# A matrix-valued causal convolution: other buffers for the first partial results

## The chip, the cores and the metric

The kernel runs on one core of a Trainium2 chip. The core has engines that run side by side, each with its own queue of instructions: TensorE (PE in the profile) multiplies matrices into PSUM, VectorE (DVE) and ScalarE (ACT) work elementwise, GpSimd (POOL) and SyncE (SP) issue transfers here. Engines wait for each other and for transfers by semaphores. The metric is the time of one execution on the device in microseconds, the median of several runs.

## The reference

```python
x: (8, 4096, 512) float32,  kernel: (8, 512, 512) float32
out = 0
for k in range(8):
    shifted = x moved down by k rows within its sequence, zeros ahead
    out += shifted @ kernel[k]
```

Each output row is the sum of eight products of a row of 512 with a 512 x 512 matrix: the row itself and the seven before it. It is a convolution along the sequence whose taps are matrices.

## The kernel before, in words

The 8 x 4096 rows are cut into 128 runs of 256 rows. A run belongs to a partition; a step is the same row of all 128 runs. Eight steps make a group, with index `i` from 0 to 31 (`NIT`), so that a group's outputs are 8 steps of 128 x 512.

The eight taps are not multiplied out one by one. A three-level scheme in the manner of Karatsuba splits taps and steps into a low and a high half at each level (`LO`, `HI`) and forms a third set (`MID`) from sums of inputs and differences of weights. Inputs are combined on VectorE in bfloat16 (`D4`, `D42`, `D421`, `D41`, `D2`, `D21`, `D1`, and in the opening `T4`, `T42`, `E4`, `F0`, `F21`, `A1`, `C0`, `C1`). A product (`product`, line 188) is 4 matmuls of 128x128 by 128x512 on one 128 x 512 half of a PSUM tile.

The work is a list of nodes, `order` (line 305). A node (i, a) is group `i` and outer level `a`; it makes the sums `p[0]` and `p[1]`, two steps each, in PSUM. On one node's way lie `node_a1`, `node_a0`, `node_u` (products in the tile `q`), ScalarE's copies of `q` as a start value (`node_seed`, lines 249 and 251) and into `dts` (line 255), `node_v` (a product each for b = 0 and 1), `node_d` (VectorE makes the other half of `p` from it, lines 263 and 265) and `node_l` (the last products). `node_e` takes the result out of PSUM. For a MID node from the third group on, ScalarE copies `p` into a tile `ms` (line 292), and the LO and HI nodes of that group add or subtract it on VectorE into a tile `y` (line 301) that is stored by SyncE (`store`, line 275).

The first six nodes go another way, since MID needs weights that come late: the order is (0, LO), (1, LO), (0, HI), (1, HI), (0, MID), (1, MID). Nodes 0 to 3 copy their `p` into tiles kept in `first` (line 288); when nodes 4 and 5 have their sums, `node_y` (line 279) adds them in place and the tiles are stored. They are stored in this order: the first group's LO and HI with b = 0 (lines 517 and 524), with b = 1 (533 and 540), then the second group's LO and HI with b = 0 (544 and 546), HI with b = 1 (556) and LO with b = 1 (559).

The tiles of `first` come from three pools (lines 194 to 197): `ms` has two buffers, `f` two, `y` four. A pool hands its buffers out in turn. Whoever takes a buffer again first waits until its last reader, here a store, is done. `f` is not used after the opening. So the pool that a node's results lie in decides on which store node 6 (the first to fill `ms` again) and nodes 7 and 8 (the first to fill `y` again) have to wait.

Everything is put in order by hand (`manual_schedule`, line 54): each engine runs its instructions in the order in which the program names them, up to line 559 one by one and from line 562 in a loop over the nodes from the seventh. SyncE issues both stores and the transposing transfers into `XT` (`transpose_x`, line 89); GpSimd loads `x` and the weights (line 80). In the opening a part of the input is transposed on TensorE instead (`transpose_pe`, line 179), and `direct(m, t)` (line 315) does the products of node 0 one by one.

Of the kernel before, what the change touches and what calls it, by code (L numbers as in the profile page):

```python
# [22 lines left out]
def kernel(  # L23
# [6 lines left out]
    nc = tc.nc  # L30
# [10 lines left out]
    ADD = mybir.AluOpType.add  # L41
# [26 lines left out]
    D21 = spool.tile([P, 4, D], bf, name="D21")  # L68
# [3 lines left out]
    F0 = spool.tile([P, D], bf, name="F0")  # L72
    A1 = spool.tile([P, 2, D], bf, name="A1")

    def tt(o, a, b, op):
        nc.vector.tensor_tensor(out=o, in0=a, in1=b, op=op)  # L76


    def load(out, src):
        nc.gpsimd.dma_start(out=out, in_=src)  # L80
# [3 lines left out]
    def load_x(i, h):  # L84
        xin[i, h] = xpool.tile([P, 4, D], bf, name="xin")
        load(xin[i, h], xr[:, K * i + 4 * h:K * i + 4 * h + 4, :])

    def transpose_x(i, h):
        nc.sync.dma_start_transpose(
            out=XT[:, 4 * h:4 * h + 4, :].rearrange("p j (c m) -> p (j c) m", m=P),  # L90
            in_=xin[i, h].rearrange("p j d -> p (j d)"))
# [20 lines left out]
    def prep_d41(h):  # L112
        if h == LO:
            tt(D41[:, 0:2], D4[:, 7::-7], D4[:, 0:2], ADD)
        else:
            tt(D41[:, 2:4], D4[:, 3:5], D4[:, 4:6], ADD)
# [18 lines left out]
    def pair(k):  # L135
        return ppool.tile([P, 2, D], f32, name=f"pp{k}")
# [4 lines left out]
    H, HF = XT, D421.bitcast(f32).rearrange("p (t b) d -> p t (b d)", b=2)  # L141
# [18 lines left out]
    def mid_dve(*which):  # L160
        o, u, v = mid(*which)
        tt(o, u, v, SUB)
# [12 lines left out]
    def transpose_pe(name, k, src, t0, t1):  # L175
        o = pair(k).bitcast(bf).rearrange("p a (b d) -> p (a b) d", b=2)
        for t in range(t0, t1):
            for c in range(DC):
                nc.tensor.transpose(o[:, t - t0, c * P:(c + 1) * P], src[:, t, c * P:(c + 1) * P],  # L179
                                    ident)  # L180
        bank[name] = o[:, 0:t1 - t0]
# [3 lines left out]
    XF = D42  # L185


    def product(bank, comp, w, start):
        for c in range(DC):
            nc.tensor.matmul(bank, lhsT=comp[:, c * P:(c + 1) * P], rhs=w[:, c, :],  # L190
                             start=start and c == 0, stop=c == DC - 1,
                             skip_group_check=True)

    mpool = ctx.enter_context(tc.tile_pool(name="m", bufs=2))
    cpool = ctx.enter_context(tc.tile_pool(name="c", bufs=2))
    fpool = ctx.enter_context(tc.tile_pool(name="f", bufs=2))
    ypool = ctx.enter_context(tc.tile_pool(name="y", bufs=4))
# [31 lines left out]
    def node_a1(k):  # L229
        n = Node()  # L230
        nodes.append(n)
        n.k, (n.i, n.a) = k, order[k]
        a = n.a
        n.s = streams(n.i, a)
        n.q = pair(3)
        product(n.q[:, 1], n.s[1][1], W[a, MID, HI], True)
        nc.scalar.copy(out=n.q[:, 0], in_=n.q[:, 1])  # L237
        n.p = {}
# [4 lines left out]
    def node_u(n):  # L243
        product(n.q[:, 1], n.s[0], W[n.a, MID, MID], False)
# [23 lines left out]
    ms = {}  # L268
# [4 lines left out]
    def store(i, a, b_, y):  # L273
        t0 = K * i + 4 * a + 2 * b_
        nc.sync.dma_start(out=orr[:, t0:t0 + 2, :], in_=y)
# [7 lines left out]
    def node_e(n, b_):  # L283
        p = n.p[b_]
        if n.k < 4:
            pool, name = ((ypool, "y"), (mpool, "ms"), (ypool, "y"), (fpool, "f"))[n.k]
            y = pool.tile([P, 2, D], f32, name=name)
            nc.scalar.copy(out=y, in_=p)
            first[n.i, n.a, b_] = y
        elif n.a == MID:  # L290
            ms[b_] = mpool.tile([P, 2, D], f32, name="ms")
            nc.scalar.copy(out=ms[b_], in_=p)  # L292
        else:
            y = ypool.tile([P, 2, D], f32, name="y")
            if b_ == HI and n.k == len(order) - 1:

                for j, eng in enumerate((nc.scalar, nc.sync)):
                    tt(y[:, j], p[:, j], ms[b_][:, j], ADD if n.a == LO else SUB)
                    eng.dma_start(out=orr[:, K * n.i + 4 * n.a + 2 * b_ + j, :], in_=y[:, j])
            else:  # L300
                tt(y, p, ms[b_], ADD if n.a == LO else SUB)
                store(n.i, n.a, b_, y)
# [12 lines left out]
    def direct(m, t):  # L315
        n = K // 2 - 1 - m
        product(n0.p[t // 2][:, t % 2], D4[:, t - m] if t >= m else E4[:, 4 + t - m],
                W[LO, n >> 1, n & 1], m == 0)


    C0, C1 = W[MID, HI, MID], W[MID, LO, MID]

    def to(z):
        return z.rearrange("p t (c m) -> p t c m", m=P)[:, :, :, 1:P]

    def prev(z):
        return z.rearrange("p t (c m) -> p t c m", m=P)[:, :, :, 0:P - 1]

    def first_run(z):

        nc.vector.memset(z[:, :, 0:D:G], 0.0)
# [2 lines left out]

    nc.vector.tensor_copy(out=H[:, 4:6], in_=HF[:, 0:2])
    nc.scalar.copy(out=H[:, 6:8], in_=HF[:, 2:4])
    n0.p = {0: pair(0), 1: pair(1)}
    load_w(6)  # L340
# [21 lines left out]
    load_x(1, 0)  # L362
    tt(to(E4[:, 1:4]), prev(bank["he"]), to(XF[:, 1:4]), ADD)
    direct(2, 2)
    direct(0, 1)
    first_run(E4[:, 1:4])
    direct(1, 1)
    tt(D1, XF[:, 3:5], XF[:, 4:6], ADD)
    mid_dve(1, LO, HI)
    nc.vector.tensor_copy(out=F0, in_=XF[:, 4])  # L370
    mid_dve(2, LO, HI)
    tt(F21, D2[:, 0:4], D2[:, 1:5], ADD)
    direct(2, 0)
# [10 lines left out]
    tt(D4[:, 4:8], XF[:, 4:8], XT[:, 4:8], ADD)  # L384
    direct(1, 2)
    tt(D42[:, 3], D4[:, 1], D4[:, 3], ADD)
    transpose_pe("x2", 2, xin[1, 0], 0, 4)
    prep_d41(HI)
    direct(3, 2)
# [10 lines left out]
    tt(D41[:, 1], T4[:, 0], T4[:, 1], ADD)  # L400
    load_w(3)
    node_a1(1)
    direct(2, 1)
    node_u(nodes[1])
    tt(D41[:, 0], D4[:, 7], T4[:, 0], ADD)
    tt(T42[:, 0:2], D4[:, 6:8], T4[:, 0:2], ADD)
# [2 lines left out]
    mid_dve(1, HI, HI)  # L409
    load_w(1)  # L410
    node_e(nodes[0], 0)
    load_x(1, 1)
    load_x(2, 0)
# [8 lines left out]
    node_seed(nodes[1], 1)  # L422
    mid_dve(1, HI, LO)
    node_e(nodes[0], 1)
    mid_dve(2, HI, HI)
    node_v(nodes[1], 1)
# [6 lines left out]
    node_a1(2)  # L433
    node_l(nodes[1], 0, LO)
    node_e(nodes[1], 0)
    transpose_x(1, 1)
    node_a0(nodes[2])
# [45 lines left out]
    node_dts(nodes[4])  # L483
    tt(D21[:, 2:4], C1[:, 0:2], C1[:, 2:4], ADD)
    mid_dve(2, MID, MID)
    tt(D21[:, 0:2], C0[:, 0:2], C1[:, 0:2], ADD)
    tt(A1[:, 1], C1[:, 0], C1[:, 1], ADD)
    load_x(3, 0)
    transpose_x(2, 0)
    mid_dve(2, MID, LO)  # L490
    node_e(nodes[3], 0)
# [148 lines left out]
```

## Time and profile before

The median of three runs is 785.68 us (783.73 to 785.83). The profiled execution took 783.4 us, of which 781.4 us are its span.

| Engine | busy, us | share of the span |
|---|---|---|
| TensorE, matmuls | 761.4 | 97% |
| VectorE | 659.6 | 84% |
| TensorE, weight loads | 346.3 | 44% |
| ScalarE | 281.9 | 36% |

| Stretch, us | TensorE busy | VectorE busy |
|---|---|---|
| 0 to 200 | 187.4 | 170.0 |
| 200 to 400 | 199.0 | 169.2 |
| 400 to 600 | 199.1 | 171.1 |
| 600 to 781 | 176.0 | 149.3 |

The granted TensorE clock is full throughout. The 16 transfer engines moved 138.9 MB, 178 GB/s in the mean. A line of the timeline gives start, duration, engine, line of the kernel, operation, output and input tile, and in brackets how long the engine had stood idle and what released it. A line of waits gives the engine and line that waited, what for, the total, the number of waits and the longest. A releaser is inferred from semaphores: where several had to come, the last is named.

### The profile page before, as it was taken

How to read it: one execution, taken by the hardware profiler on the slowest of the kernel's cores; microseconds unless marked ns; L12 is line 12 of the kernel's file. 1: busy time of each engine (PE TensorE's matmuls, PEld its weight loads, DVE VectorE, ACT ScalarE, POOL GpSimd, SP SyncE). 2: the span in 40 equal slices, each digit the busy share in tenths (PEclk: the TensorE clock that was granted, in tenths of full speed). 3: DMA queues.
4: the chain of work that ended last, by engine and by line, in shares of the span. 5: the costliest groups of instructions: out<-in, count | busy, mean ns of one | idle time of the engine just before them, and what ended most of it. 6: DMA issues, size and time to landing. Idle time of an engine off the chain costs nothing.

```text
span 781.4 us, 9358 instructions
## 1 busy us (share of the span) xinstructions
PE 761.4 (97%) x3505; PEld 346.3 (44%) x3576; DVE 659.6 (84%) x768; ACT 281.9 (36%) x460; POOL 41.3 (5%) x79
## 2 busy tenths in 40 slices
PE   7899899999999999999999999999999999999997
PEld 3444344444444444444444444444444444444443
DVE  4999888888888888888898888888888898888895
ACT  2453333333333333333323343333333333343332
POOL 4000000000000000000000000000000000000000
PEclk9999999999999999999999999999999999999999
DMA  9974878776877787777687787778797867678843
GB/s 200 211 122 137 203 178 207 159 193 163 184 170 195 177 189 170 181 181 195 155 198 173 174 186 191 190 163 181 167 193 185 195 164 183 167 189 181 203 133 123
DMA packets 159230, 138.90 MB, mean 178 GB/s; under 512 B 130129, under 2 KB 134225, under 8 KB 159057
## 3 DMA queue, kind: packets, MB, share of 16 engines
q1 hardware_dynamic: 145456, 99.89, 45.6%
q0 software_dynamic: 13584, 38.15, 30.8%
q8 instruction: 28, 0.46, 0.2%
q10 hardware_dynamic: 144, 0.26, 0.1%
q14 instruction: 18, 0.14, 0.1%
HBM read 77.33 MB, written 67.11 MB: 185 GB/s over the span
## 4 chain that ended last, share of the span: by engine, by line
PE 90%; DVE 4%; DMA 3%; issue 1%; POOL 1%; ACT 0%; DVEq 0%; ACTq 0%; POOLq 0%
PE pp L190 90%; DMA xin<-in_x_dram 2%; DVE D L76 1%; DVE w L76 1%; DMA out_dram<-ms 1%; DVE y L76 1%; POOL w L80 0%; DVE pp L76 0%; DVE pp L265 0%; ACT pp L249 0%; DVE F L76 0%; DVE XT L383 0%; DVE ms L76 0%; DVE f L76 0%; PE pp L179 0%
## 5 line engine op out<-in xcount | busy, mean ns | idle before, releaser
L190 PE MATMUL pp<-w,D 128*128 128x512 bf16 x3212 | 712.0, 379 | 10.4 <-ACT pp L249 3.0
L190 PEld LDWEIGHTS <-D 128*128 128x128 bf16 x3280 | 320.2, 98 | 395.4 <-issue 5.8
L76 DVE TENSOR_TENSOR D<-D 128x1024 bf16<-128x1024 bf16 (+1 forms) x252 | 228.4, 946 | 1.4 <-ACT D L346 1.2
L76 DVE TENSOR_TENSOR y<-pp,ms 128x1024 f32<-128x1024 f32 (+1 forms) x121 | 146.5, 1211 | 46.4 <-PE pp L190 44.9
L76 DVE TENSOR_TENSOR D<-XT 128x2048 bf16<-128x2048 bf16 (+2 forms) x153 | 142.3, 945 | 10.5 <-DMA XT<-xin 8.5
L237 ACT COPY pp<-pp 128x512 f32<-128x512 f32 x95 | 54.1, 570 | 255.1 <-PE pp L190 252.3
L249 ACT COPY pp<-pp 128x512 f32<-128x512 f32 x95 | 54.2, 570 | 170.9 <-PE pp L190 161.7
L76 DVE TENSOR_TENSOR pp<-dts,pp 128x512 f32<-128x512 f32 x95 | 65.5, 690 | 46.5 <-ACT dts L255 42.8
L292 ACT COPY ms<-pp 128x1024 f32<-128x1024 f32 x60 | 61.0, 1017 | 37.1 <-PE pp L190 30.9
L80 POOL DMA_DIRECT2D xin<-in_x_dram x64 | 34.1, 533 | 690.3 <-DMA XT<-xin 675.7
L265 DVE SCALAR_TENSOR_TENSOR pp<-pp,dts 128x512 f32<-128x512 f32 x95 | 65.8, 693 | 3.3
L255 ACT COPY dts<-pp 128x512 f32<-128x512 f32 x95 | 57.5, 605 | 2.0 <-PE pp L190 2.0
L251 ACT ACTIVATE pp<-pp 128x512 f32<-128x512 f32 x95 | 56.0, 590 | 0.8 <-DVE ms L76 0.8
L190 PE MATMUL pp<-w,XT 128*128 128x512 bf16 x118 | 30.5, 379 | 0.1
L76 DVE TENSOR_TENSOR w<-w,w 128x2048 bf16<-128x2048 bf16 x19 | 22.8, 1218 | 1.3 <-DMA w<-in_kernel_dram 1.2
L190 PEld LDWEIGHTS <-XT 128*128 128x128 bf16 x120 | 11.7, 98 | 14.2
L190 PE MATMUL pp<-w,w 128*128 128x512 bf16 x36 | 9.0, 379 | 0.7 <-ACT pp L249 0.7
L190 PE MATMUL pp<-w,F 128*128 128x512 bf16 x36 | 8.9, 379 | 0.0
L173 PE MATMUL pp<-zero 128*128 128x512 bf16 x15 | 6.2, 575 | 1.2 <-DVE zero L145 1.2
L390 ACT COPY XT<-pp 128x1024 bf16<-128x1024 bf16 x1 | 1.0, 1012 | 17.4 <-PE pp L179 17.4
L80 POOL DMA_DIRECT2D w<-in_kernel_dram x8 | 6.0, 756 | 3.9 <-DMA w<-in_kernel_dram 2.8
L190 PEld LDWEIGHTS <-w 128*128 128x128 bf16 x36 | 3.5, 98 | 5.0 <-issue 1.2
(53 smaller groups left out, 65.8 us busy)
## 6 DMA issues: line engine op xcount, KB each, us to landing
out_dram<-y SPq DMA_DIRECT2D x123, 512.0 KB, 3.4
xin<-in_x_dram POOLq DMA_DIRECT2D x64, 512.0 KB, 5.7
w<-in_kernel_dram POOLq DMA_DIRECT2D x8, 512.0 KB, 17.5
D<-in_x_dram SPq DMA_DIRECT2D x1, 1024.0 KB, 4.8
out_dram<-ms SPq DMA_DIRECT2D x2, 512.0 KB, 8.4
out_dram<-f SPq DMA_DIRECT2D x2, 512.0 KB, 8.8
XT<-xin SPq DMA_TRANSPOSE x61, 6.1
XT<-in_x_dram POOLq DMA_DIRECT2D x1, 384.0 KB, 10.5
```

Of the source, the lines that this page charges most:

```text
L76: nc.vector.tensor_tensor(out=o, in0=a, in1=b, op=op)
L80: nc.gpsimd.dma_start(out=out, in_=src)
L173: nc.tensor.matmul(pw[:, h], lhsT=zero[:, 0:P], rhs=zero, start=True, stop=True)
L190: nc.tensor.matmul(bank, lhsT=comp[:, c * P:(c + 1) * P], rhs=w[:, c, :], start=start and c == 0, stop=c == DC - 1, skip_group_check=True)
L237: nc.scalar.copy(out=n.q[:, 0], in_=n.q[:, 1])
L249: nc.scalar.copy(out=n.p[b_][:, 1], in_=n.q[:, 1])
L251: nc.scalar.mul(out=n.p[b_][:, 1], in_=n.q[:, 1], mul=-1.0)
L255: nc.scalar.copy(out=n.dts, in_=n.q[:, 0])
L265: nc.vector.scalar_tensor_tensor(out=p[:, 0], in0=p[:, 1], scalar=-1.0, in1=n.dts, op0=MUL, op1=SUB)
L292: nc.scalar.copy(out=ms[b_], in_=p)
L390: nc.scalar.copy(out=XT[:, 0:2], in_=bank["x2"][:, 0:2])
```

## The change

The results of node 0 (first group, LO) go into the buffers of `ms`, those of node 1 (second group, LO) into `y`, those of node 2 (first group, HI) into `f`, those of node 3 (second group, HI) into `y`. Before, nodes 0 and 2 were in `y`, node 1 in `ms`, node 3 in `f`. It is for the reuse: the buffers of `ms`, which are wanted again first, are now those that are stored first.

With it come four small edits of the written order: the cast of two rows of the history moves from VectorE to ScalarE; the copy into `F0` comes earlier on VectorE; the product `direct(2, 1)` comes before the transposes of `x2` on TensorE in place of behind `node_a1(1)`; and the sum into `D21[:, 0:2]` comes behind that into `A1[:, 1]`.

```diff
     def node_e(n, b_):
         p = n.p[b_]
         if n.k < 4:
-            pool, name = ((ypool, "y"), (mpool, "ms"), (ypool, "y"), (fpool, "f"))[n.k]
+            pool, name = ((mpool, "ms"), (ypool, "y"), (fpool, "f"), (ypool, "y"))[n.k]
...
-    nc.vector.tensor_copy(out=H[:, 4:6], in_=HF[:, 0:2])
+    nc.scalar.copy(out=H[:, 4:6], in_=HF[:, 0:2])
     nc.scalar.copy(out=H[:, 6:8], in_=HF[:, 2:4])
...
     direct(2, 2)
+    nc.vector.tensor_copy(out=F0, in_=XF[:, 4])
     direct(0, 1)
     first_run(E4[:, 1:4])
     direct(1, 1)
     tt(D1, XF[:, 3:5], XF[:, 4:6], ADD)
     mid_dve(1, LO, HI)
-    nc.vector.tensor_copy(out=F0, in_=XF[:, 4])
...
     tt(D42[:, 3], D4[:, 1], D4[:, 3], ADD)
+    direct(2, 1)
     transpose_pe("x2", 2, xin[1, 0], 0, 4)
...
     node_a1(1)
-    direct(2, 1)
     node_u(nodes[1])
...
     mid_dve(2, MID, MID)
-    tt(D21[:, 0:2], C0[:, 0:2], C1[:, 0:2], ADD)
     tt(A1[:, 1], C1[:, 0], C1[:, 1], ADD)
     load_x(3, 0)
+    tt(D21[:, 0:2], C0[:, 0:2], C1[:, 0:2], ADD)
     transpose_x(2, 0)
```

## The prediction

> **What bounds the kernel now.** I read the page first. Its first part says which engine fills the span:
>
> ```profile
> PE 761.4 (97%) x3505; PEld 346.3 (44%) x3576; DVE 659.6 (84%) x768; ACT 281.9 (36%) x460; POOL 41.3 (5%) x79
> ```
>
> TensorE (PE) is short of the 781.4 us span by only 20.0 us. The table by stages says where: PE is busy 187.4 us of the first 200 us, 199.0 of the next 200, 199.1 of the next. So 12.6 us of the 20 lie ahead of 200 us, and a change of the opening (which this is) can win from those alone. Next I asked what PE waited for:
>
> ```profile
> PE pp L190 <- ACT pp L249: 3.7, 2, 3.0
> PE pp L190 <- DVE D L331: 2.3, 1, 2.3
> PE pp L179 <- DMA xin<-in_x_dram: 2.1, 2, 1.6
> ...
> PE pp L179 <- DVE XT L383: 0.5, 1, 0.5
> ```
>
> Columns are total, times, longest. The largest single wait is 3.0 us for a ScalarE (ACT) seed copy of line 249. The timeline shows that it falls at 83.5 to 86.5 us, and what ScalarE did then:
>
> ```profile
> 79.29 0.57 ACT L237 COPY pp<-pp 128x512 f32<-128x512 f32 x1 [2.03 <-PE pp L190]
> 84.99 1.01 ACT L292 COPY ms<-pp 128x1024 f32<-128x1024 f32 x1 [5.12 <-DMA out_dram<-ms]
> 85.89 0.59 ACT L249 COPY pp<-pp 128x512 f32<-128x512 f32 x1
> ```
>
> The seed wasn't late by itself: it stood behind the copy of node 6's sums into `ms` (line 292), and that copy waited 5.12 us for a store out of the same `ms` buffer. The store of `first[1, LO, 0]` is issued at 76.67 us:
>
> ```profile
> 66.48 1.80 SPq L275 DMA_DIRECT2D out_dram<-y  x2
> 70.55 1.68 SPq L89 DMA_TRANSPOSE XT<-xin  x1
> 72.27 1.71 SPq L275 DMA_DIRECT2D out_dram<-y  x2
> 76.67 0.33 SPq L275 DMA_DIRECT2D out_dram<-ms  x1
> 77.05 2.29 SPq L275 DMA_DIRECT2D out_dram<-f  x2
> 80.14 0.33 SPq L275 DMA_DIRECT2D out_dram<-ms  x1
> 83.78 4.73 SPq L89 DMA_TRANSPOSE XT<-xin  x1
> ```
>
> The chain that ended last goes through that store; "issue", ACT and PE follow it:
>
> ```profile
> 75.52 1.14 DVE ms L76
> 76.66 0.02 issue
> 76.67 8.23 DMA out_dram<-ms
> ```
>
> It lands at 76.67 + 8.23 = 84.90 us. Two facts for later: the `y` stores of the opening are issued 4 to 10 us before it, and VectorE (DVE) has no gap over 0.1 us from 63.5 to 85.5 us, so it becomes the next suspect once this wait is gone.
>
> [...] three instructions at 84.99, 85.89 and 86.41 us run back to back after one wait, though only the first needed the store. [...] between 76 and 83 us DMA moves 310 to 420 GB/s.
>
> **The change, part by part.**
>
> *Buffers (line 286).* Node 0's two results go to `ms`, node 1's to `y`, node 2's to `f`, node 3's to `y`. Node 6 then reuses `ms` after the stores of `first[0, LO, *]`. The first is issued at 66.48 us; the longest landing of any `y` store here is 5.9 us, so it is free by 72.4 us. Node 6's copy is ready when its second product is done, at about 81 us: margin over 8 us. The second is issued by 74 us, free by 80, wanted after 86. This removes the 3.02 us of PE idle.
>
> The wait could come back where the late buffers go. Nodes 7 and 8 take the four `y` buffers in the order in which nodes 1 and 3 took them. VectorE writes node 7's first `y` at 91.92 us now, 88.9 after (3.0 earlier), into the buffer stored at 76.67 and landed at 84.9: margin 4.0. Its second is written at 98.26 now, 95.2 after, into the one stored at 80.14; with the 8.6 us of that store it lands at 88.7: margin 6.5. Node 8's buffers are stored between 77.05 and 79.3, landing within 9.1 us. None waits. Cost zero; what would queue behind such a wait is all of VectorE.
>
> *What VectorE and the transposes allow.* Without the wait PE does the first product of line 258 for node 7 at 83.5 us. VectorE finishes its backlog at 85.5, so the difference of node 7 ends at 86.2, and PE wants it four products later (0.864 us each, from 4 matmuls at 0.216): 83.5 + 3.5 = 87.0. It holds, by 0.8 us. The next test is the transpose issued at 83.78 us, whose release is the VectorE read at 82.48, not PE; it won't come earlier. It took 7.4 us to land here, so 91.2 us. `prep_m` stands on VectorE just behind node 7's first `y`, so it could start at 90.0 and will wait until 91.2. Behind it are 1.73 us of `prep_m`, 1.14 of `prep_d421`, 0.69 of node 8's difference: 94.76 us. PE reaches the product that needs it 13 products after 83.52, at 94.75. It fits to a hair; I take 0.1 us of loss, between 0 (transpose lands as the median 6.1 us) and 1.5 (lands 1.4 later than here).
>
> *`direct(2, 1)` earlier (4 matmuls, 0.86 us).* It goes from behind `node_a1(1)` to ahead of the transposes of `x2`. There PE idles 0.45 us for the PSUM bank:
>
> ```profile
> 26.99 1.05 PE L179 MATMUL pp<-ident,xin 128*128 128x128 bf16 x16 [0.45 <-DVE XT L383]
> 28.08 1.01 ACT L390 COPY XT<-pp 128x1024 bf16<-128x1024 bf16 x1 [17.41 <-PE pp L179]
> 28.99 1.02 ACT L392 COPY XT<-pp 128x1024 bf16<-128x1024 bf16 x1
> 30.19 1.22 DVE L76 TENSOR_TENSOR w<-XT 128x2048 bf16<-128x2048 bf16 x1
> ```
>
> Four matmuls from 26.60 end at 27.46, so the transposes come 0.47 us later, the two ScalarE copies too, and line 392's ends at 30.48 in place of 30.01. The sum into `T4` on VectorE started at 30.19, so it slips by about 0.3 us. From there to 46 us VectorE has hardly a gap, and PE takes up its results at 38.1 and at 46.1 (there PE idled 0.35 us already). So the 0.86 us that PE saves behind 32 us turn into waiting for VectorE, and the 0.3 us stay. Bounds: 0 (the opening has other slack) and 0.5 (all of the shift). I take 0.3 us added.
>
> *The cast of line 337 to ScalarE.* Two casts one after the other on ScalarE end at about 6.6 and 7.55 us (5.58 start, 0.95 pitch of these 1.05 us rows), where the second ended at 6.6. The copy of line 343 starts at 7.55 in place of 7.21. The next one, line 346, starts at 8.75, after transposes that wait for `xin`, so about 0.05 us is passed on. All of it is hidden at 24.61 us, where PE stands 1.58 us for a load issued at 5.94. Zero.
>
> *`F0` earlier, 0.29 us on VectorE.* It delays the following sums by 0.29 us until 17.1; the next instruction waits until 18.48 for a weight load (1.05 us idle). Zero. *`D21[0:2]` behind `A1[:, 1]`:* two sums of 0.68 and 0.41 us change places near 60 us; PE has no gap there from 52.7 to 83.5 us. Zero.
>
> *Sum:* -3.0 + 0.1 + 0.3 + 0 = -2.6 us.
>
> **The rivals.**
>
> *Partial gain.* The 94.75 against 94.76 us above leaves nothing for a slower transpose, and the 3.02 us are worth only what comes ahead of it. If it lands 1.4 us later, or `T4`'s slip grows to 0.5, -2.6 becomes about -1.2 us: 784.4. For it: VectorE is busy 15.7 of the 16 us from 92 to 108 us. Against: the transpose would have had less traffic with it if anything.
>
> *The wait moves.* If the late stores landed 4 us later still, node 7's `y` on VectorE would wait, differences would be late and PE stop as before: -3.0 + 3.0 + 0.3, so 786.0. Against: margins of 4.0 and 6.5 us.
>
> *Slower.* VectorE, now 3 us behind where it was against PE, might not catch up, and each of the 29 remaining groups of 8 steps could lose about 0.2 us at the transposed input: 29 x 0.2 - 2.6 = +3.2, so 788.9. For it: VectorE waited seven times for transposed input, up to 1.8 us. Against: in steady state it stands idle waiting for PE at the `y` sums (44.9 us in 60 waits), which is room to catch up, and PE is at 199 of 200 us there.
>
> **How the numbers follow.** Forecast 0.60, partial gain 0.22, wait moved 0.10, slower 0.08. The time before spreads: the three runs gave 783.73, 785.68 and 785.83, the profiled one 783.4. From the median, 785.68 - 2.6 = 783.1; from the mean of the four, 784.66 - 2.6 = 782.1. I take the middle, 782.6. Low end: if the waiting store is what spreads the runs (2 us more in the longer ones), the change removes that too: 783.4 - 2.6 = 780.8, less 0.4 for the bounds at zero, 780.4. High end: the partial gain plus 1 us of spread, 785.4. The bound for faster is 783.3. The forecast falls beyond it in about 9 of 10, the partial gain in 4 of 10: 0.63. Slower by 0.3% (788.0): 0.09. Same: 0.28.
>
> **What the changed profile would show.** The line of waits "PE for ACT line 249" keeps 0.7 us at most, and no copy into `ms` waits for a store; PE runs through 83.5 to 86.5 us. `T4`'s sum starts near 30.5. `prep_m` near 90 us waits for a transpose. No `y` sum waits for a store. The forecast is wrong if PE has a new wait over 1 us between 84 and 110 us, if PE is below 199 of 200 us after 200 us, or if the opening up to 52 us is longer by over 0.5 us.

## The result and the profile after

The changed kernel takes 780.41 us in the median of four runs (780.05 to 780.85), the kernel before 785.41 us in four (783.73 to 785.83). The ratio is 0.9941, with a 95% interval of 0.9923 to 0.9958: faster by 0.6%, or 5.0 us. The prediction had 782.6 us and a range from 780.4 to 785.4. The direction and the place were right; the gain was nearly twice the forecast one, so that the measured time lies at the very edge of the range. The two profiled executions, 783.4 and 780.21 us, differ by only 3.2 us, and their spans, 781.4 and 778.4, by 3.0. So the profile of before that the prediction read was one of the shorter executions, and about 2 us of the gain can't be seen by comparing these two.

First what the pair of profiles shows. What TensorE waited for in the changed kernel (total, times, longest):

```profile
PE pp L190 <- DMA w<-in_kernel_dram: 2.6, 1, 2.6
...
PE pp L190 <- ACT pp L237: 0.7, 1, 0.7
PE pp L190 <- ACT pp L249: 0.7, 1, 0.7
```

The wait of 3.0 us for line 249 is gone; only the 0.7 us near 36 us is left of that line. The first line isn't new: it is the same instruction near 11 us that stood 2.3 us in the profile of before, with another releaser named. ScalarE at the place of the old wait:

```profile
79.27 0.57 ACT L237 COPY pp<-pp 128x512 f32<-128x512 f32 x1 [2.03 <-PE pp L190]
80.94 1.01 ACT L292 COPY ms<-pp 128x1024 f32<-128x1024 f32 x1 [1.10 <-PE pp L190]
82.67 0.57 ACT L249 COPY pp<-pp 128x512 f32<-128x512 f32 x1 [0.71 <-PE pp L190]
```

Line 292 starts at 80.94 us in place of 84.99, as soon as TensorE has the sums, and the seed of line 249 follows at 82.67. SyncE's stores explain it; the stores out of the `ms` buffers are now issued at 66.45 and 72.26 us, and the late ones, the second group's, come out of `y`:

```profile
66.45 0.35 SPq L275 DMA_DIRECT2D out_dram<-ms  x1
...
72.26 1.22 SPq L275 DMA_DIRECT2D out_dram<-ms  x1
...
76.65 3.79 SPq L275 DMA_DIRECT2D out_dram<-y  x4
83.75 4.92 SPq L89 DMA_TRANSPOSE XT<-xin  x1
```

The four late stores are no quicker than before: 8.4 to 9.3 us to landing. Nobody waits for them any more. TensorE, first before, then after the change (start, duration):

```profile
86.54 13.98 PE L190 MATMUL pp<-w,D 128*128 128x512 bf16 x63 [3.02 <-ACT pp L249]
100.36 1.03 PE L190 MATMUL pp<-w,XT 128*128 128x512 bf16 x4
```

```profile
77.29 20.03 PE L190 MATMUL pp<-w,D 128*128 128x512 bf16 x92
97.15 1.03 PE L190 MATMUL pp<-w,XT 128*128 128x512 bf16 x4
```

It now runs through, and the matmuls with `XT` come at 97.15 us in place of 100.36. And VectorE, the suspect for what comes next:

```profile
88.71 1.22 DVE L76 TENSOR_TENSOR y<-pp,ms 128x1024 f32<-128x1024 f32 x1 [0.56 <-PE pp L190]
90.78 1.83 DVE L76 TENSOR_TENSOR D<-XT 128x1024 bf16<-128x1024 bf16 x2 [0.85 <-DMA XT<-xin]
92.53 1.22 DVE L76 TENSOR_TENSOR D<-D 128x2048 bf16<-128x2048 bf16 x1
93.66 0.68 DVE L76 TENSOR_TENSOR pp<-dts,pp 128x512 f32<-128x512 f32 x1
```

Node 7's `y` waits for TensorE and for no store; `prep_m` waits 0.85 us for the transpose; node 8's difference ends at 94.34 us, and TensorE doesn't stop for it.

### The profile page after: what moved, and what is told of

It reads as the page before. It is cut to its first block, busy times and chain, and to the rows that moved or that the text cites. A ratio compares the mean times of both kernels' runs of the same rounds, so it can differ in the third digit from the quotient of the medians.

```text
span 778.4 us, 9432 instructions
## 1 busy us (share of the span) xinstructions
PE 765.6 (98%) x3576; PEld 346.9 (45%) x3576; DVE 658.7 (85%) x767; ACT 282.7 (36%) x461; POOL 41.2 (5%) x79
## 4 chain that ended last, share of the span: by engine, by line
PE 92%; DVE 4%; DMA 2%; issue 1%; POOL 1%; DVEq 0%; ACT 0%; ACTq 0%; POOLq 0%
PE pp L190 92%; DMA xin<-in_x_dram 2%; DVE w L76 2%; DVE D L76 1%; POOL w L80 0%; DVE pp L76 0%; DVE pp L265 0%; DVE XT L383 0%; PE pp L179 0%; DVE y L76 0%; DVE A L76 0%; POOL xin L80 0%; DVEq L635 0%; ACT pp L249 0%; POOL XT L80 0%
```

## The experiments

"Before" is the median of the kernel before on the same chip, measured beside the run.

**Which part of the change it is.** `e1` takes the kernel before and changes the pools alone; `e2` makes the four small edits alone.

```diff
e1:
-            pool, name = ((ypool, "y"), (mpool, "ms"), (ypool, "y"), (fpool, "f"))[n.k]
+            pool, name = ((mpool, "ms"), (ypool, "y"), (fpool, "f"), (ypool, "y"))[n.k]
e2 (on the changed kernel):
-            pool, name = ((mpool, "ms"), (ypool, "y"), (fpool, "f"), (ypool, "y"))[n.k]
+            pool, name = ((ypool, "y"), (mpool, "ms"), (ypool, "y"), (fpool, "f"))[n.k]
```

> The kernel before with only the line of the four pools changed, none of the small edits of the order. Theory (the wait for the store is all of the gain): 780.4 us within 0.6, ratio 0.994; TensorE's wait of 3.0 us for line 249 near 84 us is gone, and no copy into ms waits for a store. Rival (the small edits bring a share, for instance the 2 us between 783.5 and 785.7 us over which the kernel before spreads): 782 to 783 us, with that spread still there.

Measured: 779.93 us against 785.62 before, ratio 0.9941 (0.9924 to 0.9959). The single line is all of the gain.

> The changed kernel with the four pools as they were before, so only the small edits of the order. Theory: as before, 785.4 us, ratio 0.998 to 1.002, with the 3.0 us wait near 84 us. Rival (the edits bring a share): 783.4 us or less, ratio under 0.998.

Measured: 785.46 us against 785.62, ratio 0.9999 (0.9988 to 1.0011). The four edits are worth nothing that can be measured, the spread included.

**Which store the copy waits for.** Two more assignments on the kernel before:

```diff
e3:
+            pool, name = ((ypool, "y"), (fpool, "f"), (mpool, "ms"), (ypool, "y"))[n.k]
e4:
+            pool, name = ((ypool, "y"), (fpool, "f"), (ypool, "y"), (mpool, "ms"))[n.k]
```

> The kernel before with another assignment: node 0 in y, node 1 in f, node 2 in ms, node 3 in y. The ms buffers are then those of the first group's HI results, stored at about 68 and 73.5 us. Theory (all that counts is that the buffer which node 6 takes is stored early): 780.4 us within 0.6, ratio 0.994, no wait of ScalarE for a store. Rival (it is the assignment of the change as such, or its y buffers): 782 us or more.

Measured: 779.92 us, ratio 0.9942 (0.9926 to 0.9958), and no copy into `ms` waits for a store. It isn't this assignment that counts, but that node 6's buffer is one that is stored early.

> The kernel before with node 1 in f and node 3 in ms, so that node 6's copy waits for the store of the second group's HI results, issued about 0.4 us later than the one it waited for before, and with up to 9.1 us to landing. Theory: the wait grows with that store's landing, TensorE idles 3.5 to 4.2 us there, 786 to 786.6 us, ratio 1.000 to 1.002. Rival (which store it is makes no difference to TensorE): the same 3.0 us of idle time as before.

Measured: 786.93 us, ratio 1.0026 (1.0013 to 1.0039): slower, as expected, but by more than the 786.6 us and 1.002 at the end of the expected range. In its profile, ScalarE and TensorE:

```profile
85.91 1.01 ACT L292 COPY ms<-pp 128x1024 f32<-128x1024 f32 x1 [6.48 <-DMA out_dram<-ms]
```

```profile
87.46 16.68 PE L190 MATMUL pp<-w,D 128*128 128x512 bf16 x64 [4.38 <-ACT pp L249]
```

TensorE's gap follows the landing of the store: 4.38 us here (3.5 to 4.2 were expected), 3.02 before, none in `e3`. The theory of the wait holds in both directions. But the figures don't add up yet: the gap grows by 1.4 us, and against the short executions of before (783.3 us, see below) the time grows by 3.6.

**What VectorE would allow.** `e5`, `e8` and `e6` put one, two and three more sums of 128 x 2048 (1.13 us each) ahead of node 7's differences in the changed kernel. Their result is not used.

```diff
             prep_d41(HI)
+            if k == 6:
+                for _ in range(1):
+                    tt(F21[:, 0:4], D42[:, 0:4], D42[:, 0:4], ADD)
```

> The changed kernel with one more VectorE sum of 128 x 2048 (1.13 us from start to start, into a tile no longer read) just ahead of node 7's differences. Theory (VectorE reaches that difference about 0.8 us ahead of TensorE's need, as predicted): TensorE loses 1.13 - 0.8 = 0.3 us, once; 780.4 + 0.3 = 780.7 us. Rival (VectorE is the bound once the store's wait is gone): the whole 1.1 us, 781.5. Second rival (VectorE has slack to spare there): nothing, 780.4.

Measured: 781.06 us, 0.65 above the changed kernel's 780.41, which was taken separately. TensorE's gap for VectorE's difference in the profile is 0.33 us, as expected from a slack of 0.8 us. There is a second wait for line 249, of 0.2 us (0.9 in two, the longest 0.7), and TensorE is busy for 99.75 of the 100 us from 600 to 700 us, where the changed kernel's has no gap; so not all of it came at once.

> The same with three such sums, 3.4 us. Theory: 3.4 - 0.8 = 2.6 us lost, once, and nothing later: 783.0 us. Rival (VectorE the bound): 3.4 us and more, since the backlog is carried on: 783.8 or more. Second rival (slack to spare): under 1 us, 781.4 or less.

Measured: 785.09 us, ratio to before 1.0007. The gap is the expected one:

```profile
PE pp L190 <- DVE pp L76: 2.9, 1, 2.9
```

The time is not: 4.7 us are lost with a gap of 2.85. By the number alone the rival "VectorE the bound" would have won (783.8 or more), but its cause, a backlog carried on, isn't there: TensorE has no other gap from 70 to 110 us. Three of the 14 executions, those with a mean clock of 1.000, took 783.35 to 783.74 us; the others, with 0.993 to 0.997, 784.94 to 785.9.

**Where the other 2 us go.** `e2`'s profile happened to be a longer execution, 785.82 us. What each engine did in stretches of 2 us: the busy time of TensorE, its weight loads, VectorE, ScalarE and GpSimd, each with its number of instructions as (x...); behind them TensorE's granted clock, the busy share of the transfer engines and their GB/s. First the kernel before as the prediction read it, then `e2`, which is the same there:

```profile
86.00:88.00 2.00, 1.46 (x7) 0.68 (x7) 0.33 (x1) 1.49 (x3) 0.00 (x0) 1.00 1.46 241
88.00:90.00 2.00, 2.00 (x11) 0.89 (x10) 1.90 (x3) 0.00 (x0) 0.00 (x0) 1.00 1.14 200
90.00:92.00 2.00, 2.00 (x11) 0.94 (x10) 0.70 (x3) 1.50 (x2) 0.28 (x1) 1.00 0.07 4
```

```profile
86.00:88.00 2.00, 1.02 (x4) 0.43 (x4) 0.09 (x1) 1.93 (x4) 0.00 (x0) 0.83 1.35 359
88.00:90.00 2.00, 2.00 (x6) 0.64 (x5) 0.70 (x1) 0.00 (x0) 0.00 (x0) 0.50 0.96 78
90.00:92.00 2.00, 2.00 (x9) 0.88 (x8) 1.72 (x2) 0.00 (x0) 0.00 (x0) 0.81 0.64 143
```

TensorE comes back from the gap, is "busy" all the time, and does 6 matmuls in 2 us in place of 11, at a clock of 0.50. From the end of the gap to the matmuls with `XT` before takes 100.36 - 86.54 = 13.82 us, `e2` 102.49 - 86.98 = 15.51: 1.7 us lost. In `e4`, behind 4.38 us of gap, it is 103.97 - 87.46 = 16.51, so 2.7 lost. The profile of `e6` shows the same as `e2`: the clock is 0.50 from 90 to 92 us, right behind its gap.

The kernel before was measured beside each set of runs, in 73 executions, each with its mean clock. In 21 this is 0.999 or 1.000: 782.68 to 784.44 us, median 783.3. In 52 it is 0.992 to 0.998: 783.57 to 786.73, median 785.6, all but one above 784.3. So the time goes with the clock. But the mean of an execution doesn't say where the clock was lower: in some executions it falls in the opening too, also in kernels without the gap (0.50 from 12 to 14 us in the changed kernel's profile). Whether it is this gap that counts is for `e7` to show.

How long the slow stretch in `e2` lasted can be estimated from its clocks above: 0.83, 0.50 and 0.81 lack (0.17 + 0.50 + 0.19) x 2 us of the full one, which at a clock of 0.50 makes 3.4 us. The gap ahead of it is 2.88 us long in `e2` and 2.85 in `e6`.

`e8` has a gap between those of `e5` and `e6`:

> The changed kernel with two more VectorE sums of 128 x 2048 ahead of node 7's differences, which makes an idle gap of TensorE of about 0.33 + 1.13 = 1.5 us. If a gap of that length leaves the clock alone: 780.4 + 1.5 = 781.9 us, spread about 1 us, as with one sum. If it costs the clock as the gaps of 2.9 us do: 783.5 us or more in most executions, with a spread of 2 us or more.

Measured: 782.17 us (781.67 to 782.85), gap 1.59 us, clock 1.00 from 78 to 150 us. The unaltered changed kernel on the same chip:

> The changed kernel once more, unaltered, on the chip of the two runs above, for comparison with them: 780.4 us within 0.6.

Measured: 780.26 us (779.63 to 780.93). So 1.9 us are lost with a gap of 1.59: a gap of this length costs about itself. (The mean of the whole profiled execution is 0.995; it is low from 12 to 20 us, in the opening.)

`e7` keeps the wait of the kernel before and fills TensorE's gap. The 14 matmuls add products with zeros to a sum.

```diff
     load_x(3, 0)
+    z2 = spool.tile([P, P], bf, name="z2")
+    nc.gpsimd.memset(z2, 0.0)
...
+        if k == 6:
+            for _ in range(14):
+                nc.tensor.matmul(cur.p[1][:, 1], lhsT=z2, rhs=W[LO, LO, LO][:, 0, :],
+                                 start=False, stop=False, skip_group_check=True)
         if nxt:
             for b_ in range(2):
                 node_v(nxt, b_)
```

> The kernel before, its wait for the store kept, with 14 matmuls of zeros put on TensorE just where it would stand idle (14 x 0.216 = 3.0 us; they add zero to a sum). Theory (an idle gap of about 3 us costs itself and, in most executions, some 2 us more, since TensorE comes back at half the clock for some us): TensorE is not idle, so the clock stays full and every execution takes what the undisturbed ones of the kernel before take, 783.3 us within 0.7, spread under 1.5 us, granted clock of the later part 1.00. Rival (the spread of the kernel before comes from the store's landing or from other transfers): 785.4 us with a spread of 3 us, as before.

Measured: 783.36 us (782.57 to 784.27, 14 executions) against 785.01 before, ratio 0.9980 (0.9972 to 0.9988). ScalarE still waits 5.0 us for the store, and the useful work goes on no earlier than before:

```profile
83.47 3.19 PE L596 MATMUL pp<-w,z 128*128 128x512 bf16 x14
86.56 13.98 PE L190 MATMUL pp<-w,D 128*128 128x512 bf16 x63
```

The 63 matmuls take 13.98 us, just what they took in the profiled execution of before at full clock. Matmuls of no use make the kernel 1.65 us faster, because they keep the clock: it is 1.00 in every stretch from 82 to 100 us, where `e2` had 0.83, 0.50 and 0.81. The rival, a later landing of the store, would have left the time at 785. It also separates the opening: ten of the 14 executions still have a mean clock under 0.999, and in the profiled one it is 0.98 up to 12 us, 0.63 from 12 to 16, and 1.00 from 16 to 24 and from 78 to 150; yet none takes over 784.27 us, less than 51 of the 52 executions of before with a lower clock. The spread is 1.7 us, a little over the 1.5 expected.

**The gap of the opening.** `e10` adds five calls of `fill(pair(1))`, two matmuls each, ahead of `direct(0, 0)` in `e1`, where TensorE stands 2.2 us near 10 us; `e11` is `e1` again on the same chip.

> The kernel with only the four pools changed, and ten matmuls of zeros (2.2 us) on TensorE ahead of the first product of node 0, where TensorE stands 2.2 to 2.6 us for a weight load near 10 us. Theory (that gap too leads to half the clock in some executions, from about 12 to 18 us, which mostly ends within the wait for a load at 24.5 us): the granted clock is 0.999 or 1.000 in all or nearly all executions, and the time stays 779.4 to 780.1 us, 0 to 0.5 us below the run beside it. Rival (the clock in the opening has nothing to do with that gap): the clock still varies from 0.994 to 1.000, no change of time.

Measured: 780.02 us, clock 0.998 to 1.000 in all six executions.

> The kernel with only the four pools changed once more, unaltered, on the same chip as the run with the filled opening: 779.9 us within 0.6, granted clock 0.994 to 1.000 from one execution to the next.

Measured: 779.93 us, clock 0.995 to 1.000 in five; in its profile the clock is 0.57 from 12 to 20 us. Filling the gap steadies the clock and wins nothing in the median. The profiles say why in part: at full clock TensorE stands 0.72 us for a load until 23.96 us (`e10`, the opening filled); in `e11`'s, slow from 12 to 20 us, that wait is gone and the same work begins at 25.21. So a part of what is lost ahead of this place, 0.72 us by these two profiles, is hidden there; why the rest doesn't show in the median stays open. No version tried is measurably better than the changed kernel or `e1`.

## Why the prediction was right, and where it wasn't

*The wait, its length and its end.* Right: the 3.02 us of TensorE's gap are gone, by the pools alone (`e1`, `e2`), and the gap follows the store (`e3`, `e4`). The matmuls with `XT` come 100.36 - 97.15 = 3.21 us earlier.

*What it is worth: the mis-sized term.* The sum had "-3.0" for it: a gap was priced at its length. Shown in its place: the gap and the half clock behind it, 1.7 us in `e2`'s profile, which by clock and time came in 51 of the 73 executions of before. `e7`, which keeps the one and removes the other, divides them on one chip: 785.01 before, 783.36 with the gap filled, 780.26 for the changed kernel (`e9`). So 1.65 us are the clock and 3.10 the gap, 4.75 together; in the result it was 785.41 - 780.41 = 5.0. The profile at hand had a full clock, so this couldn't be read from it; the spread of the runs was the sign.

*Why the range still held: luck.* The prediction saw the four times of before spread by 2.4 us and guessed that the store landed later in some. Its low end, 780.4, rests on this guess, and the measured 780.41 lies on it. `e7` refutes the guess, as filling the gap would not have helped then. The range held for a wrong reason.

*Why the store is late.* The prediction read 310 to 420 GB/s between 76 and 83 us. That is a wrong reading: in the profile of before the transfers moved 49 to 274 GB/s from 76 to 82 us and 401 to 434 only from 82 to 86. From 77 to 82 us a load of `x` on GpSimd's queue took 87.7% of the transfer engines' time, and SyncE's queue with the stores 6.6%. The late stores took 8.2 to 9.1 us to landing, where the page's median of the `y` stores is 3.4. So the stores seem to have stood behind that load; this is an estimate from these shares, and no run tests it.

*The wait doesn't move to `y`.* Right. Node 7's `y` was predicted at 88.9 and started at 88.71, waiting for TensorE.

*VectorE's slack of 0.8 us.* Right: 1.13, 2.26 and 3.39 us of added work gave gaps of 0.33, 1.59 and 2.85 in the profiles, so 0.8, 0.7 and 0.5 us of slack.

*The transpose.* Predicted: `prep_m` held until 91.2 us and 0.1 us lost. It started at 90.78 and TensorE lost nothing; the transpose took 7.0 us in place of 7.4. (In the rival "partial gain" the -1.2 us follow from a slower transpose alone; a slip of `T4` by 0.5 us would have made -2.4.)

*`direct(2, 1)`: +0.3 us, wrong.* `T4`'s sum was to slip from 30.19 to about 30.5. The changed kernel:

```profile
25.41 1.03 PE L190 MATMUL pp<-w,D 128*128 128x512 bf16 x4
...
26.28 1.03 PE L190 MATMUL pp<-w,w 128*128 128x512 bf16 x4
...
27.14 1.06 PE L179 MATMUL pp<-ident,xin 128*128 128x128 bf16 x16
...
29.14 1.02 ACT L393 COPY XT<-pp 128x1024 bf16<-128x1024 bf16 x1
...
30.19 1.23 DVE L76 TENSOR_TENSOR w<-XT 128x2048 bf16<-128x2048 bf16 x1
```

It starts at 30.19 as before; the transposes came 0.15 us later, not 0.47. The prediction had started the added product at 26.60, behind a product that its trace showed from 25.73 with three matmuls. A product has four: a record was missing, and by the changed kernel's trace it was the first (there the product comes 0.90 us behind the start of the transposes, before 1.12), so the product had ended 0.2 us earlier than read. And the changed execution had reached this place 0.1 us earlier (24.51 against 24.61). ScalarE's copy of line 393 ends at 30.16, just before VectorE is free for the sum, so the delay stayed within the slack. That TensorE saves nothing behind 32 us fits `e2`'s 0.9999.

*Cast, `F0`, `D21`: nothing.* Right for all four edits together, by the same 0.9999; none was run alone.

## What to carry to other kernels

When partial results are parked in pools that the steady loop uses too, sort them by when they will be stored: the buffers that the loop takes first should hold what is stored first. Price an idle gap of the matmul engine near 3 us at more than its length, by the granted clock in the stretches behind it (here 3.10 us for the gap and 1.65 for the clock); and where the runs of one kernel spread, ask for the clock of each before taking one profile for the typical one. Where such a gap can't be removed, matmuls of zeros in it may pay, as in `e7` (1.65 us).

## What the runs showed of the hardware

Between dense matmuls, a gap of TensorE of 2.85 us (`e6`) and one of 2.88 us (`e2`) brought the half clock in the profiles, one of 3.02 us (the kernel before) did not. By the times it came in about 7 of 10 executions: 51 of 73 of the kernel before have a lower mean clock and lie above 784.3 us, 11 of 14 of `e6` have one and lie above 784.9. Behind 4.38 us it came in `e4`'s profile; and all ten executions of `e4`, from 786.08 us on, lie above 783.3 + 1.4 = 784.7 us, an estimate for a full clock from the short executions of before and the longer gap. Behind 0.33 and 1.59 us the clock stayed full in the one profile of each. In the opening, a gap of 2.2 us did it in `e11`'s profile, with smaller gaps around it, and not in `e1`'s. The half clock lasted 3.4 us in `e2` and `e6`, and 6.8 us in `e4`, where it had begun inside the gap (0.53 from 86 to 88 us, of which the first 1.46 are gap); these lengths are estimates from the clocks in stretches of 2 us. It cost 1.7 and 2.7 us in `e2` and `e4`. What decides in which execution a gap of 2.9 us does it was not tried.
